# Third token mixer: when its tiles are fetched, which queue issues two of its loads, and which engines copy and scale

## The chip, the cores and the metric

The kernel runs on one core of one Trainium2 chip. The metric is device time in microseconds, the median over runs. The engines that the text names are TensorE (PE), VectorE (DVE), ScalarE (ACT), GpSimd (POOL) and SyncE (SP), which here only issues DMAs. Each engine works through a fixed list of its own instructions in order.

## The reference

Two layers, 512 latent tokens (x) and 256 context tokens (z), width 1024, all in float32. Each layer is a modulated RMSNorm, one wide input projection, three token mixers side by side, gated projections of the three outputs, an output projection and a SwiGLU feed-forward. The change is in the third mixer, a bidirectional recurrence with one 64 x 64 state for each of 8 heads:

```python
def step(S, inp):
    w_t, k_t, v_t, kk_t, a_t = inp[:5]
    sa = jnp.einsum('bhvk,bhk->bhv', S, kk_t)
    S = S * w_t[:, :, None, :] - sa[..., None] * (kk_t * a_t)[:, :, None, :] + v_t[..., None] * k_t[:, :, None, :]
    return S, jnp.einsum('bhvk,bhk->bhv', S, inp[5])
```

It is run over the context first and then over the latent tokens, once forward and once on the reversed sequence; context outputs are needed in the first layer only.

## The kernel before

Matrices stand with features on the partitions. Every float32 product of a large projection is made of three matmuls of a high and a low part (`gemm`); weights come as `raw` tiles from SP, are split into `wh` on ACT and `wl` on DVE (`wunit`), and are used up as "jobs".

The third mixer (`Rwkv.run`) treats the 768 tokens as six stretches of 128 tokens, called halves in the code's words, for each of two directions, `f` and `b`. Two generators ("lanes"), one for a direction, are stepped in turn, and jobs of other work (gates, then the projections of the first two mixers) are put between the steps. For each half and direction there are three stages:

- `prep(d, g)` loads `cp` (log decays), `bk` and `kr` (keys, replacement vectors, receptances) from DRAM over SP, makes cumulative decays (a DVE scan, two ACT exponentials), scales `kr` and `bk` by them (`kr[..., 0:32]` and `bk` on DVE, `kr[..., 32:64]` at L1479 and the final decay `pc` into `bk` at L1498 on POOL), makes score matrices `X` on TensorE, and transposes `bk` into `bkt`.
- `inverse(d, g)` writes parts of `X` to DRAM (`d1`), reads them back as `L`, loads an identity `G`, solves 31 elimination steps of two instructions each (DVE for `f`, POOL for `b`), writes `G` to DRAM (`d2`) and reads it back as `TT`. All these DMAs are SP's.
- `chain(it)` runs four chunks of 32 tokens. For each: `yp` on TensorE from `uv`, `X`, `kr` and the state; `ysb` on ACT; the solve `up` = `TT` times `ysb`; four copies of `up` into `uv`, two on DVE and two on ACT in turn (L1593); `sp` from `uv` and `bkt`; the new state `sblk` on DVE (L1606), for which POOL scaled the old one (`sc`); and, where outputs are needed, `op` and its copy `ys`. The values `uv` come from DRAM over SP, in two loads for each half (L1553).

The first layer runs `prep` and `inverse` one half ahead of the chain, the second two halves ahead (`self.ahead`). The rotating buffers decide when a load may start: `kr` has 6, `cp`, `bk`, `G` and `L` have 2 each for both directions together, `uv` has 2 for each direction. A load into a buffer that is still read waits on its queue, and what stands behind it on that queue waits too.

The code is written in program order, but the order of the instructions on each engine is made by the framework's scheduler at build time, from that order and from its own estimate of times. In the second layer `paced` also ties the jobs' matmuls to the steps of the chain.

Of the kernel before, what the change touches and what calls it, by code (L numbers as in the profile page):

```python
# [20 lines left out]
KD = 8  # L21
# [3 lines left out]
FREE, PER = 150, 3.3  # see paced()  # L25
# [3 lines left out]
class Kern:  # L29
# [18 lines left out]
    # ---------------------------------------------------------------- helpers  # L48
# [35 lines left out]
    def hop(self, i):  # L84
        """a product of a chain that others are paced by"""
        if self.hops is not None:
            self.hops.append(i)

    def paced(self, i, ps):
        """beside a chain: the first FREE products (of 512 columns) as they come, then at most PER more after each one of the chain,  # L90
        so that those of the chain never queue behind many others"""
        if self.hops is not None:
            if self.done >= FREE and self.hops:
                self.after(i, self.hops[min(int((self.done - FREE) / PER), len(self.hops) - 1)])
            self.done += ps.shape[-1] / 512

    def room(self, n):
        """whether n more products fit the pace"""
        return self.done + n <= FREE + PER * len(self.hops)
# [10 lines left out]
    def run_job(self, later=None):  # L110
        """the next queued job; what a job returns is its second half, left to the caller if `later` is a list"""
# [14 lines left out]
    def rsqrt(self, y, s, t):  # L126
        """y = s ** -0.5 (s, y, t: same-shape SBUF tiles)"""
# [7 lines left out]
    def rsqrt_v(self, y, s, t):  # L135
        """y = s ** -0.5 without table functions: a guess from the halved exponent, three Newton steps"""
# [9 lines left out]
    # ---------------------------------------------------------------- consts  # L146
# [32 lines left out]
    # ---------------------------------------------------------------- adaLN  # L179
    def ada(self, l, bank, R, rbufs):  # L180
        """generator: modulation vectors of layer l, one round per 2048 columns; bank(shape, name): a PSUM tile, R: pool of the weights"""
# [36 lines left out]
    # ---------------------------------------------------------------- norm  # L218
    def stats(self, xk, a, b, P, tags, S, y):
        """generator: y <- 1 / rms of the tokens a..b-1 (rows 32 j: j-th quarter); P, tags: PSUM pool and (tag, bufs) of its one-bank tiles;  # L220
        S: pool of temporaries"""
# [18 lines left out]
    def spread(self, y, n, P, tags, S):  # L240
        """the n values of y, over all partitions (PSUM)"""
# [9 lines left out]
    def norm(self, xk, a, b, P, tags, S, apply):  # L251
        """generator: rmsnorm of the tokens a..b-1; apply(k, r): emits what follows for the k-th feature tile, r: 1 / rms over all partitions"""
# [10 lines left out]
    # ---------------------------------------------------------------- mixer input  # L263
    def gemm_x(self, w):
        """one 128-column tile of the input projection of the x tokens, feature-major"""
# [15 lines left out]
    def new_h(self, Z=None):  # L281
        """tiles of the two parts of h; Z: pool of the z tokens, where they lie apart"""
# [3 lines left out]
    def h(self, j, k, a, b):  # L286
        """part j (high, low) of the tokens a..b-1 of h, k-th feature tile"""
        return self.hz[j][k][:, a - NX:b - NX] if self.hz and a >= NX else self.hs[j][k][:, a:b]

    def norm_mod(self, xk, a, b, A, sh, P, tags, S, y=None):  # L290
        """generator: h = rmsnorm(x) * g * (1 + scale) + shift of the tokens a..b-1, split into two float32r parts;
        y: the tokens' 1 / rms, where they are known"""
# [21 lines left out]
    # ---------------------------------------------------------------- layers  # L314
    @contextmanager
    def weights(self, name, bufs, side=None):
        """pool of the weight tiles of the jobs to come; raw ones of their own only at the outermost level"""
# [14 lines left out]
    def fill(self):  # L332
        """one queued job, if any"""
# [6 lines left out]
    def mixed(self, gen, steps, spread):  # L340
        """run the mixer `gen` (about `steps` steps) with the queued jobs spread over it"""
# [9 lines left out]
    def layer(self, l, X, xs):  # L351
# [76 lines left out]
        with self.pool(f"pf{l}", space=PSUM) as pg:  # L428
# [5 lines left out]
            # layer 1: paced by the chain; layer 0, where TensorE is the bound: evenly from the start  # L434
# [30 lines left out]
        # merge, output projection, feed-forward  # L465
# [30 lines left out]
    def branch_jobs(self, l, n):  # L496
        """gated output projections of the first two mixers, summed into accd"""
# [24 lines left out]
    # tokens in two groups: those whose third mixer output comes last (0..127, 384..511) and the others  # L522
# [8 lines left out]
    def branch_operand(self, l, late, raw):  # L531
        """the third mixer's output of one group of tokens, in two parts"""
# [6 lines left out]
    def branch_gemm(self, l, w, m, late, g):  # L539
        """g <- gated product of one group of tokens"""  # L540
# [6 lines left out]
    def last_branch(self, l, n, P):  # L547
        """the third mixer's projection of the first group, added to what accd holds: the first group's operand of the output projection"""
# [18 lines left out]
    def gemm_parts(self, w, nk, rh, rl, parts):  # L567
        """products of the tokens of each part: (PSUM, first token, end)"""
# [51 lines left out]
    def two_parts(self, xs, parts, update, norm, keep=6):  # L620
        """the last KD queued jobs for the first part of the tokens, then for the second, with the first part's norm beside them;
        returns the second part's norm, not yet finished"""
# [25 lines left out]
    def ffn(self, l, n, xs):  # L648
# [3 lines left out]
        with self.ps, self.pool(f"fA{l}") as A:  # L652
# [27 lines left out]
            # the last update in two parts of the tokens, each part's norm as soon as it is there  # L680
# [19 lines left out]
            # the first tiles while the second part's norm is finished  # L700
# [22 lines left out]
    def final(self, xs, a, b, N, S):  # L723
        """generator: the final norm of the tokens a..b-1"""
# [30 lines left out]
# ------------------------------------------------------------------ gated linear attention  # L755
class Gla:
    """one layer's bidirectional gated linear attention; chunks of 128 tokens: x 0..3, z 4..5"""
# [77 lines left out]
    def cum(self, hp):  # L835
        """per-chunk cumulative log gates (times 16) of both directions for head pair hp"""
# [21 lines left out]
    def states(self, hp, B):  # L858
        """scaled queries, and the state before every chunk, of both directions"""
# [164 lines left out]
# ------------------------------------------------------------------ windowed attention  # L1024
class Swa:
    """one layer's grouped-query attention; tile t holds heads t and t + 4, key-value head g the rows 64 g"""

    def __init__(self, K, l, P, ps, yb):
# [13 lines left out]
        # float32r parts: a head's queries as (high; low) in one order of the row halves, keys twice  # L1042
# [5 lines left out]
    def add_jobs(self, P):  # L1048
        """projection jobs; P: pool of what only they need"""
# [46 lines left out]
    def run(self, T):  # L1096
# [4 lines left out]
        # the softmax of one group of heads beside the value products of the group before  # L1101
# [13 lines left out]
    def values(self, T, n, g, keys, r):  # L1115
        """generator: transposes of the weights, value products of one group of heads; its output when both groups are there"""
# [99 lines left out]
# ------------------------------------------------------------------ RWKV-7  # L1216
class Rwkv:
    """one layer's RWKV-7 mixer; tokens: x 0..511, z 512..767; halves of 128 tokens: x 0..3, z 4..5"""
# [9 lines left out]
    def open_f(self):  # L1228
        """what the projection jobs need"""
# [15 lines left out]
        self.hb = P.tile([128, 16], F32, name="hb")  # half of w0 (f p0..3, b p0..3), a0  # L1245
# [43 lines left out]
    # -- evacuation of a projected tile with the centred shift mix  # L1289
# [10 lines left out]
    def add_jobs(self, J, ps, psn):  # L1300
        """projection jobs; J: pool of temporaries, ps/psn: PSUM pool and (tag, bufs) of its one-bank tiles"""
# [14 lines left out]
        def lowrank(half, di, p, t):  # L1316
            """tanh of half the low-rank product plus half the offset"""
# [36 lines left out]
        def keys(p):  # L1354
            """normalised keys, and the two directions' replacement vectors and keys, of head pair p"""
# [67 lines left out]
    def knorm(self, J, bank, big, kt):  # L1423
        """1 / max(|k * k_k|, 1e-12) per head: rows 32 (token block) + head, columns x 0..127, z 128..191"""
# [23 lines left out]
    # -- decays and scores of 128 tokens of one direction  # L1448
    def prep(self, d, g):
        nc, K, T, ps = self.nc, self.K, self.T, self.ps  # L1450
        di = "fb".index(d)
        c4 = slice(4 * g, 4 * g + 4)
        outp = self.need_out(g)
        nI = 64 if outp else 32
# [4 lines left out]
        nc.sync.dma_start(cp.rearrange("q (p c) t -> q p (c t)", c=4), row(self.twd[d]))  # L1459
        nc.sync.dma_start(bk.rearrange("q (p w) c t -> q p (w c t)", w=2), row(self.bkd[d]))  # L1460
        nc.sync.dma_start(kr.rearrange("q (p c) t -> q p (c t)", c=4), row(self.krd))
# [16 lines left out]
        if outp:  # L1478
            nc.gpsimd.tensor_tensor(out=kr[:, :, 32:64], in0=kr[:, :, 32:64], in1=Pi, op=ALU.mult)  # L1479
        yield  # L1480
        # transposed scores, rows (even chunk: B~ j, k~ j; odd chunk: k~ j, B~ j), columns (K~ i, r~ i)
# [14 lines left out]
        v = bk.rearrange("q (p w) (c h) t -> q p (w c) (h t)", w=2, h=2)  # L1496
        for p in range(4):
            nc.gpsimd.tensor_tensor(out=v[:, p], in0=v[:, p], in1=pc[:, p, :].unsqueeze(2).to_broadcast([128, 4, 64]), op=ALU.mult)  # L1498
# [9 lines left out]
    def inverse(self, d, g):  # L1508
# [274 lines left out]
def _layout(x, c, ctx, c_ctx, w_ada, b_ada, g_mix, g_ffn, w_in, w_gk2, b_gk, g_gla, sink, mu_shift, w0, w_w2, a0, w_a2,  # L1783
            w_g2, k_k, k_a, r_k, gn_w, gn_b, w_branch, w_out, w_ffn1, w_ffn3, w_ffn2, g_final):
    f = np.float32
    D = {}
# [74 lines left out]
```

## Time and profile before

| | |
|---|---|
| median of 3 runs | 3359.13 us (3357.03 to 3359.63) |
| profiled execution, first to last instruction | 3361.6 us |
| TensorE busy | 3033.8 us (90%), mean granted clock 0.921 |
| VectorE, ScalarE, GpSimd busy | 1756.6, 1081.2, 990.4 us |
| third mixer, first layer | about 640 to 1165 us of the span |
| third mixer, second layer | about 2436 to 2871 us of the span |

The profiled execution has no time of its own on record other than its span, which stands 2.5 us above the median of the runs. A busy share is a mean over stages; the two stretches of the third mixer have their own.

### The profile page before, as it was taken

Reading aid. Unit: us, or ns where it says so; the run is one execution under the profiler, and the core shown is the slowest. Engines: PE = TensorE matmul, PEld = TensorE weight load, DVE = VectorE, ACT = ScalarE, POOL = GpSimd, SP = SyncE. Lnnn points to the kernel's source line nnn. Section 1 sums busy time; section 2 is a strip of 40 time slices with the busy share of each in tenths; the row PEclk is TensorE's granted clock in tenths of the full one; section 3 lists DMA queues with packets and bytes.
Section 4 is the critical chain, followed back from the end, with each engine's and each line's share of the span. In section 5 each row is a group of like instructions: output and inputs, shape, how many; then the busy total and the mean of one; then the engine's idle time right before and its main releaser. Section 6 shows DMA issues by size and latency. Waiting matters only on the chain. (4 is left out here: it accounts for less than half of the span.)

```text
span 3361.6 us, 62705 instructions
## 1 busy us (share of the span) xinstructions
PE 3033.8 (90%) x25760; PEld 2400.0 (71%) x25760; DVE 1756.6 (52%) x3506; ACT 1081.2 (32%) x2034; POOL 990.4 (29%) x1438
## 2 busy tenths in 40 slices
PE   6999999878889989999999899698857789799998
PEld 3777877666666778888888787576635466788887
DVE  3175557766656755222223454656567566643335
ACT  3255444422222233212122344453322222332223
POOL 2033122344655322101001211312266465221102
PEclk9999999888888999999999899798868679899999
DMA  7421222544345552443212322123633444512223
GB/s 289 153 74 56 96 101 95 174 131 124 99 119 142 168 197 73 153 157 132 63 63 95 96 73 95 58 76 126 205 103 107 112 131 137 187 69 95 96 98 119
DMA packets 269375, 398.33 MB, mean 118 GB/s; under 512 B 94624, under 2 KB 179360, under 8 KB 269088
## 3 DMA queue, kind: packets, MB, share of 16 engines
q1 hardware_dynamic: 249184, 370.20, 34.2%
q10 hardware_dynamic: 19904, 24.12, 2.0%
q8 instruction: 202, 3.31, 0.4%
q14 instruction: 85, 0.70, 0.1%
HBM read 320.33 MB, written 73.92 MB: 117 GB/s over the span
## 5 line engine op out<-in xcount | busy, mean ns | idle before, releaser
L50 PE MATMUL px<-hh,wl 128*128 128x512 f32 x1584 | 646.5, 408 | 31.9 <-DVE wl L72 31.8
L50 PE MATMUL px<-hh,wh 128*128 128x512 f32 x1584 | 651.9, 412 | 14.1 <-ACT wh L71 6.5
L50 PE MATMUL px<-hl,wh 128*128 128x512 f32 x1584 | 643.2, 406 | 11.6 <-POOL hl L302 8.8
L72 DVE TENSOR_TENSOR wl<-raw,wh 128x1024 fp32r<-128x1024 f32 (+1 forms) x314 | 402.3, 1282 | 366.4 <-ACT wh L71 332.1
L71 ACT ACTIVATE wh<-raw 128x1024 fp32r<-128x1024 f32 (+1 forms) x314 | 326.1, 1041 | 778.8 <-PE pz L50 395.2
L50 PEld LDWEIGHTS px<-hh,wl 128*128 128x128 f32 x1584 | 308.2, 195 | 110.0 <-DVE wl L72 38.1
L50 PEld LDWEIGHTS px<-hh,wh 128*128 128x128 f32 x1584 | 309.4, 195 | 106.7 <-issue 24.4
L50 PEld LDWEIGHTS px<-hl,wh 128*128 128x128 f32 x1584 | 308.8, 195 | 82.3 <-POOL hl L302 13.2
L673 POOL TENSOR_TENSOR al<-fs,ah 128x768 fp32r<-128x768 f32 (+1 forms) x44 | 85.0, 1931 | 726.3 <-ACT ah L672 726.3
L50 PE MATMUL pz<-hl,wh 128*128 128x256 f32 x872 | 253.1, 291 | 3.8 <-DVE hl L304 2.0
L50 PE MATMUL pz<-hh,wh 128*128 128x256 f32 x872 | 253.5, 292 | 1.5 <-DVE fs L663 1.4
L50 PE MATMUL pz<-hh,wl 128*128 128x256 f32 x872 | 252.0, 289 | 1.3 <-DVE wl L72 0.8
L50 PEld LDWEIGHTS pz<-hl,wh 128*128 128x128 f32 x872 | 171.2, 196 | 10.4 <-POOL hl L302 2.6
L50 PEld LDWEIGHTS pz<-hh,wh 128*128 128x128 f32 x872 | 170.3, 196 | 11.2 <-issue 3.2
L50 PE MATMUL px<-y,wh 128*128 128x512 f32 (+1 forms) x512 | 155.8, 391 | 24.8 <-ACT y L123 10.0
L50 PEld LDWEIGHTS pz<-hh,wl 128*128 128x128 f32 x872 | 170.4, 195 | 7.0 <-issue 5.2
L1532 POOL TENSOR_TENSOR ftmp<-G,L 128x60 f32<-128x60 f32 (+24 forms) x372 | 125.9, 338 | 146.9 <-DMA G<-gid 55.8
L1532 DVE TENSOR_TENSOR ftmp<-G,L 128x60 f32<-128x60 f32 (+24 forms) x372 | 107.4, 289 | 103.8 <-DMA G<-gid 55.6
L1533 POOL TENSOR_TENSOR G<-G,ftmp 128x60 f32<-128x60 f32 (+24 forms) x372 | 131.4, 353 | 25.2
L50 PE MATMUL sp<-uv,bkt 64*64 64x64 f32 x1536 | 99.8, 249 | 36.9 <-DVE uv L1593 36.5
L50 PEld LDWEIGHTS px<-y,wh 128*128 128x128 f32 x512 | 96.1, 209 | 44.2 <-ACT y L123 12.5
L50 PEld LDWEIGHTS sp<-uv,bkt 64*64 64x64 f32 x1536 | 69.3, 147 | 75.4 <-DVE uv L1593 41.1
(443 smaller groups left out, 6090.9 us busy)
## 6 DMA issues: line engine op xcount, KB each, us to landing
raw<-win SPq DMA_DIRECT2D x114, 512.0 KB
raw<-w SPq DMA_DIRECT2D x104, 512.0 KB
araw<-wada SPq DMA_DIRECT2D x96, 512.0 KB
raw<-w SPq DMA_DIRECT2D x48, 448.0 KB
kr<-krd SPq DMA_DIRECT2D x24, 512.0 KB
L<-d SPq DMA_DIRECT2D x24, 512.0 KB
gs<-gat ACTq DMA_DIRECT2D x24, 384.0 KB
raw<-wab SPq DMA_DIRECT2D x16, 512.0 KB
```

What stands on the lines that cost most here:

```text
L50: return self.nc.tensor.matmul(out, lhsT=lhsT, rhs=rhs, start=start, stop=stop)
L71: nc.scalar.activation(h[:, :n], raw[:, :n], AF.Copy)
L72: nc.vector.tensor_tensor(out=lo[:, :n], in0=raw[:, :n], in1=h[:, :n].bitcast(F32), op=ALU.subtract)
L673: nc.gpsimd.tensor_tensor(out=al, in0=s, in1=ah.bitcast(F32), op=ALU.subtract)
L1532: eng.tensor_tensor(out=t, in0=G[:, rows, j:j + 1].to_broadcast([128, a, m]), in1=L[:, j:j + 1, cols].to_broadcast([128, a, m]), op=ALU.mult)
L1533: eng.tensor_tensor(out=G[:, rows, cols], in0=G[:, rows, cols], in1=t, op=ALU.subtract)
```

## The change

`load` takes the three loads out of `prep`. The first half's loads stand at the start of `run`, the later ones in `inverse` of the half before, behind its `L`; `kr` now goes ahead of `bk`. `load_v` takes the `uv` loads out of `chain`, one window of 64 tokens at a time, after the first and the third chunk of each half, and issues them from ACT's queue. `G` is loaded from ACT's queue too. All four copies of `up` are ACT's. The two scalings that were POOL's for both directions are DVE's for `f` and POOL's for `b`, and the scaling by `pc` is one instruction where it was four. The diff also drops comments and docstrings.

```diff
+    def load(self, d, g):
+        nc, T = self.nc, self.T
         c4 = slice(4 * g, 4 * g + 4)
         cp = T.tile([128, 16, 34], F32, name="cp", tag="cp", bufs=2)
         kr = T.tile([128, 16, 64], F32, name="kr", tag="kr", bufs=6)
         bk = T.tile([128, 8, 4, 32], F32, name="bk", tag="bk", bufs=2)
         row = lambda a: a[:, :, c4, :].rearrange("q p c t -> q p (c t)")
         nc.sync.dma_start(cp.rearrange("q (p c) t -> q p (c t)", c=4), row(self.twd[d]))
+        nc.sync.dma_start(kr.rearrange("q (p c) t -> q p (c t)", c=4), row(self.krd))
         nc.sync.dma_start(bk.rearrange("q (p w) c t -> q p (w c t)", w=2), row(self.bkd[d]))
-        nc.sync.dma_start(kr.rearrange("q (p c) t -> q p (c t)", c=4), row(self.krd))
+        self.loaded[d, g] = cp, kr, bk
+    def load_v(self, d):
+        if self.windows[d]:
+            g, w = self.windows[d].popleft()
+            uv = self.uvs[d, g, w] = self.T.tile([128, 4, 2, 64], F32, name="uv", tag="uv" + d, bufs=2)
+            v0 = 128 * g + 64 * w
+            self.nc.scalar.dma_start(uv[32:96].rearrange("q p e v -> q (p e v)"), self.vtok[v0:v0 + 64, :])
     def prep(self, d, g):
+        eng = nc.vector if d == "f" else nc.gpsimd
+        cp, kr, bk = self.loaded.pop((d, g))
...
         if outp:
-            nc.gpsimd.tensor_tensor(out=kr[:, :, 32:64], in0=kr[:, :, 32:64], in1=Pi, op=ALU.mult)
+            eng.tensor_tensor(out=kr[:, :, 32:64], in0=kr[:, :, 32:64], in1=Pi, op=ALU.mult)
...
-        v = bk.rearrange("q (p w) (c h) t -> q p (w c) (h t)", w=2, h=2)
-        for p in range(4):
-            nc.gpsimd.tensor_tensor(out=v[:, p], in0=v[:, p], in1=pc[:, p, :].unsqueeze(2).to_broadcast([128, 4, 64]), op=ALU.mult)
+        v = bk.rearrange("q a (c h) t -> q (a c) (h t)", h=2)
+        eng.tensor_tensor(out=v, in0=v, in1=pc.rearrange("q p c -> q (p c)").unsqueeze(2).to_broadcast([128, 16, 64]), op=ALU.mult)
...
-    def inverse(self, d, g):
+    def inverse(self, d, g, later):
...
+        if later is not None:
+            self.load(d, later)
         G = T.tile([128, 8, 32], F32, name="G", tag="G", bufs=2)
-        nc.sync.dma_start(G, self.I["gid"])
+        nc.scalar.dma_start(G, self.I["gid"])
...
     def chain(self, it):
-        uvs = {}
-        for w in ((0, 1) if d == "f" else (1, 0)):
-            uv = uvs[w] = T.tile([128, 4, 2, 64], F32, name="uv", tag="uv" + d, bufs=2)
-            v0 = 128 * g + 64 * w
-            nc.sync.dma_start(uv[32:96].rearrange("q p e v -> q (p e v)"), self.vtok[v0:v0 + 64, :])
...
             for p in range(4):
-                o, i_ = uv[ru, p].rearrange("q e v -> q (e v)"), up[32 * p:32 * p + 32, :]
-                (nc.scalar.copy if p % 2 else nc.vector.tensor_copy)(o, i_)
+                nc.scalar.copy(uv[ru, p].rearrange("q e v -> q (e v)"), up[32 * p:32 * p + 32, :])
...
+            if n % 2 == 0:
+                self.load_v(d)
...
     def run(self):
+        for d in "fb":
+            self.load(d, seqs[d][0])
+            self.windows[d] = deque((g, w) for g in seqs[d] for w in ((0, 1) if d == "f" else (1, 0)))
+        for d in "fb":
+            self.load_v(d)
```

Two places show how the scheduler's order moves. The first is SP's list in the second layer, around the end of the chain's first half. The `kr` rows here load the fourth half of each direction and wait until the chain has left the first half; `d2` and `TT` are the way of the second half's solves, forward first (in the rows of before `TT_23584` and `TT_23601`). Before:

```order
L1461 DMA kr_24337<-krd1_20782 128x4x256
L1518 DMA L_23828<-d1_23824 128x1x1024
L1461 DMA kr_24373<-krd1_20782 128x4x256
L1536 DMA d2_23456<-G_23467 4x256x32
L1459 DMA cp_25061<-twdf1_20783 128x4x136
L1518 DMA L_23863<-d1_23859 128x1x1024
L1536 DMA d2_23462<-G_23486 4x256x32
L1553 DMA uv_24317<-vtok1_20789 64x512
L1538 DMA TT_23584<-d2_23456 128x8x32
L1521 DMA G_23923<-gid 128x256
```

Now, from the corresponding stretch of the changed kernel, where `TT_23552` and `TT_23569` are the second half's:

```order
L1532 DMA L_23774<-d1_23770 128x1x1024
L1552 DMA d2_23412<-G_23429 4x256x32
L1554 DMA TT_23552<-d2_23412 128x8x32
L1532 DMA L_23809<-d1_23805 128x1x1024
L1552 DMA d2_23418<-G_23454 4x256x32
L1554 DMA TT_23569<-d2_23418 128x8x32
L1457 DMA kr_23870<-krd1_20746 128x4x256
L66 DMA raw_24459<-win 128x1024
L1457 DMA kr_23935<-krd1_20746 128x4x256
```

Both `TT` loads now stand directly behind their `d2` writes (one `L` between the two pairs), with no `uv`, `cp` or `G` between them; the two waiting `kr` loads moved behind them.

The second place is ACT's list in the second layer at the chain's first chunk, where the first copies of `up` stand. Before:

```order
L1505 COPY bkt_23728<-tp_23818 128x512
L1505 COPY bkt_23794<-tp_23847 128x512
L1593 COPY uv_23603<-up_23663 32x128 x2
L1505 COPY bkt_23794<-tp_23853 128x512
L1593 COPY uv_23633<-up_23729 32x128
L1467 ACTIVATE cp_24372<-cs_24378 128x544
L1593 COPY uv_23633<-up_23729 32x128
L1574 ACTIVATE ysb_23808<-yp_23795 128x128
```

Now, with the `G` loads of the second half's solves ahead of the copies:

```order
L1537 DMA G_23429<-gid 128x256
L1482 ACTIVATE cp_23869<-cs_24294 128x544
L1537 DMA G_23454<-gid 128x256
L1483 ACTIVATE cs_24294<-cs_24294,lnh_65 128x544
L1603 COPY uv_22801<-up_23611 32x128 x4
L1603 COPY uv_22803<-up_23676 32x128 x4
L1585 ACTIVATE ysb_23754<-yp_23741 128x128
```

All eight copies of a chunk pair are ACT's now, and DMA issues that may wait for a buffer (`G_23429` and `G_23454` take the buffers of the first half's `G`, once `d2` has been written from them) stand in the same list.

## Rows read from the trace of the kernel before

**Rows 1.** The page's first line.

```profile
span 3361.6 us, 62705 instructions
```

**Rows 2.** Windows: stretch, length, busy PE, PEld, DVE, ACT, POOL, PE clock, DMA.

```profile
640.00:1165.00 525.00, 458.54 (x5954) 342.68 (x5951) 327.10 (x807) 138.14 (x330) 262.07 (x541) 0.88 0.46 134
2436.00:2871.00 435.00, 343.45 (x4621) 231.82 (x4619) 270.99 (x703) 104.67 (x259) 244.32 (x524) 0.76 0.41 116
2774.00:2845.00 71.00, 70.96 (x1080) 46.48 (x1082) 42.11 (x101) 19.50 (x56) 34.03 (x59) 0.93 0.42 135
```

**Rows 3.** Waits of PE, 640 to 1165: us in total, times, longest.

```profile
PE sp L50 <- DVE uv L1593: 31.6, 7, 8.7
PE px L50 <- DVE wl L72: 11.6, 9, 6.7
PE xp L50 <- DVE bk L1477: 10.0, 2, 5.6
...
PE up L1584 <- DMA TT<-d: 3.7, 2, 2.1
```

**Rows 4.** Waits of PE, 2436 to 2871.

```profile
PE up L1584 <- DMA TT<-d: 27.4, 4, 16.2
PE px L50 <- DVE wl L72: 17.7, 4, 10.8
PE xp L50 <- POOL kr L1479: 11.9, 2, 7.3
...
PE up L1584 <- ACT ysb L1574: 5.0, 2, 4.8
```

**Rows 5.** Timeline of SP's queue, second layer: start, us until issued, instruction.

```profile
2541.50 0.58 SPq L1536 DMA_DIRECT2D d<-G  x1
...
2553.30 8.73 SPq L1553 DMA_DIRECT2D uv<-vtok  x1
2562.12 0.53 SPq L1538 DMA_DIRECT2D TT<-d  x1
```

**Rows 6.** Timeline of SP's queue, a hundred us later.

```profile
2661.76 0.54 SPq L1536 DMA_DIRECT2D d<-G  x1
2673.60 0.39 SPq L1538 DMA_DIRECT2D TT<-d  x1
```

**Rows 7.** Waits on SP's queue, 640 to 1165.

```profile
SPq L1553 <- PE op L1611: 50.2, 15, 12.8
SPq L1538 <- DMA d<-G: 40.7, 11, 11.5
```

**Rows 8.** Waits on SP's queue, 2436 to 2871.

```profile
SPq L1538 <- DMA d<-G: 35.1, 9, 11.2
...
SPq L1553 <- PE op L1611: 22.7, 6, 10.1
```

**Rows 9.** Waits of DVE, 2436 to 2871.

```profile
DVE ftmp L1532 <- DMA G<-gid: 42.9, 4, 21.0
```

**Rows 10.** Tile uv: its copies and loads, ns min/median/max.

```profile
L1593 DVE COPY uv<-up x192: 268/284/292, 738.5 to 2864.0; 32x128 f32<-32x128 f32 x192
L1593 ACT COPY uv<-up x192: 254/257/262, 738.8 to 2864.3; 32x128 f32<-32x128 f32 x192
L1553 SPq DMA_DIRECT2D uv<-vtok x48: 494/554/8792, 656.6 to 2823.2; - x48
```

**Rows 11.** Tile kr: its two scalings, ns min/median/max.

```profile
L1475 DVE TENSOR_TENSOR kr<-kr,cp x24: 674/686/2140, 655.2 to 2710.4; 128x512 f32<-128x512 f32 x24
L1479 POOL TENSOR_TENSOR kr<-kr,cp x20: 1176/1218/2158, 653.0 to 2711.2; 128x512 f32<-128x512 f32 x20
```

**Rows 12.** Tile bk: its two scalings.

```profile
L1498 POOL TENSOR_TENSOR bk<-bk,pc x96: 607/612/1678, 661.0 to 2730.1; 128x256 f32<-128x256 f32 x96
L1477 DVE TENSOR_TENSOR bk<-bk,cs x24: 1206/1228/2221, 653.7 to 2658.2; 128x1024 f32<-128x1024 f32 x24
```

**Rows 13.** Waits of POOL, 640 to 1165.

```profile
POOL kr L1479 <- ACT cp L1467: 27.4, 4, 10.7
```

More of the change, by code (lines that the diff above doesn't have):

```diff
@@ L1446, in need_out @@
         return g < 4 or self.zout
-    def prep(self, d, g):
-        nc, K, T, ps = self.nc, self.K, self.T, self.ps
-        di = "fb".index(d)
+    def load(self, d, g):
+        nc, T = self.nc, self.T
         c4 = slice(4 * g, 4 * g + 4)
-        outp = self.need_out(g)
-        nI = 64 if outp else 32
         cp = T.tile([128, 16, 34], F32, name="cp", tag="cp", bufs=2)
@@ L1459, in prep @@
         nc.sync.dma_start(cp.rearrange("q (p c) t -> q p (c t)", c=4), row(self.twd[d]))
+        nc.sync.dma_start(kr.rearrange("q (p c) t -> q p (c t)", c=4), row(self.krd))
         nc.sync.dma_start(bk.rearrange("q (p w) c t -> q p (w c t)", w=2), row(self.bkd[d]))
-        nc.sync.dma_start(kr.rearrange("q (p c) t -> q p (c t)", c=4), row(self.krd))
+        self.loaded[d, g] = cp, kr, bk
[5 more added lines that the diff above has]
+            self.nc.scalar.dma_start(uv[32:96].rearrange("q p e v -> q (p e v)"), self.vtok[v0:v0 + 64, :])
+    def prep(self, d, g):
+        nc, K, T, ps = self.nc, self.K, self.T, self.ps
+        di = "fb".index(d)
+        eng = nc.vector if d == "f" else nc.gpsimd
+        outp = self.need_out(g)
+        nI = 64 if outp else 32
+        cp, kr, bk = self.loaded.pop((d, g))
         flat = lambda a: a.rearrange("q a b -> q (a b)")
@@ L1556, in chain @@
             w, q = cl // 2, cl % 2
-            S, uv = self.st[d], uvs[w]
+            S, uv = self.st[d], self.uvs[d, g, w]
             rv = slice(32, 64) if q == 0 else slice(64, 96)
@@ L1667, in run, with front @@
         done, tails = set(), []
-        def front(d, g):
-            yield from self.prep(d, g)
-            yield from self.inverse(d, g)
+        self.loaded, self.windows, self.uvs = {}, {}, {}
+        def front(d, i):
+            yield from self.prep(d, seqs[d][i])
+            yield from self.inverse(d, seqs[d][i], seqs[d][i + 1] if i < 5 else None)
+        seqs = {d: [g for x, g in self.ORDER if x == d] for d in "fb"}
+        for d in "fb":
[3 more added lines that the diff above has]
+            self.load_v(d)
         def lane(d):
-            seq = [g for x, g in self.ORDER if x == d]
+            seq = seqs[d]
             for i in range(self.ahead):
-                for _ in front(d, seq[i]):
+                for _ in front(d, i):
                     yield
             for i, g in enumerate(seq):
-                nxt = front(d, seq[i + self.ahead]) if i + self.ahead < 6 else iter(())
+                nxt = front(d, i + self.ahead) if i + self.ahead < 6 else iter(())
                 it = dict(d=d, g=g, ys=None)
```

## Prediction

> **What bounds the kernel now.** I read the windows over the two stretches of the third mixer first, then who TensorE waits for in each, then the SP queue, since SP is what the change touches most. In the first layer the mixer takes 525 us, of which TensorE is idle 525.0 - 458.5 = 66.5, at a mean granted clock of 0.88; in the second it takes 435 us, idle 91.5, clock 0.76 [rows 2]. The reader is to see that both stretches have TensorE as the engine that does most, and that in neither is it full: 158 us of idle time in all. A third row says where the floor is: from 2774 to 2845, when no half border and no front of a later half is in the way, TensorE is busy 70.96 of 71 us. There a faster chain would buy nothing. So the change can win only what waits cost elsewhere, and the slower clock that comes with them.
>
> The waits of TensorE have different ends. In the first layer the largest is `sp` behind the DVE copies of `up`, 31.6 us in 7 places [rows 3]: the copy itself is 0.28 us [rows 10], so DVE was held by something else in its list. In the second layer it is `up` behind the landing of `TT`, 27.4 us in 4 places, the longest 16.2, which is the start of the chain [rows 4]. Behind `TT` stands SP. At one border of halves `d2` was issued at 2541.5 and `TT` at 2562.1 [rows 5]; at another place, with nothing between them, the same pair is 11.84 us apart, and that is what the write to DRAM takes until it is seen [rows 6]. So at the first place `TT` could have gone at 2541.5 + 11.84 = 2553.3, and it went 8.8 us later; the row between them is a `uv` load that sat 8.73 us on SP for its buffer.
>
> **What the change removes.** The `uv` loads leave SP. Their waits there for `op` are 50.2 us in 15 places in the first layer and 22.7 in 6 in the second [rows 7, 8]; most are hidden, because what stands behind them is not due. By rows 4 I count what is not: of the 27.4 us of `TT` the 16.2 stay (the first half's solve has no chain before it to hide in), the other 11.2 go, since `TT` now stands directly behind `d2`. In the first layer, of 3.7, I take 2.
>
> *DMA: Bandwidth & Descriptors* of the Trainium skill, section "Issuing engines are not separate DMA queues", says that starting DMAs from several engines saves only the sequencer's time to initiate them, usually small beside the DMA. The trace shows something else on this queue, the wait in rows 5, which is 16 times the median issue of 0.554 us in rows 10. By the page the move is worth nothing on the path and its place in the sum would be 0 where I have 13.2.
>
> The copies leave DVE. With four in turn on two engines they cost 2 x 0.284 + 2 x 0.257 = 1.08 us a chunk, on ACT alone 4 x 0.257 = 1.03 [rows 10]: nothing by themselves. What goes is the wait on a held DVE. But the state update that follows is DVE's too, so it is still late; only the copy and `sp` come out from under it. I take half of the 31.6 us of the first layer, 16; all of it would be the upper bound, 0 the lower. In the second layer, 5 for `ysb` and the like [rows 4].
>
> The scalings move. For `f`, 12 halves lose 4 x 0.612 = 2.45 us each on POOL and 10 lose 1.218, in all 41.6 us; DVE gets 12 x 1.228 + 10 x 0.686 = 21.6 us (priced by its own scalings of the same shapes) and loses 192 x 0.284 = 54.5 [rows 10 to 12]. ACT gets 192 x 0.257 = 49.3 us and 72 DMA issues, at SP's 0.554 us 40 at most. DVE has 525 - 327 and 435 - 271 us of room, ACT more [rows 2], so the moved work is hidden. What counts is that POOL, in order, stood at `f`'s work: `kr` there waited 27.4 us for ACT's exponentials [rows 13] with `b`'s solve behind it. In the second layer TensorE waits 11.9 us for that same POOL instruction [rows 4]; the load under it still waits for a buffer, so I take half, 6.
>
> *SBUF — State Buffer* of the Trainium skill, section "Who interferes with whom", says that a DVE instruction with two SBUF inputs and a GpSimd instruction that reads SBUF contend, one blocking until the other ends. That speaks against giving `f`'s products to DVE while POOL solves `b`. The trace agrees that such pairs stretch: 1.228 us becomes 2.221 at worst, 0.612 becomes 1.678 [rows 12]. By the page the 22 new DVE instructions could cost up to 22 x (1.678 - 0.612) = 24 us, an estimate, and the sum would be 42 instead of 66.
>
> In the sum I take 0 for this stretching: 22 instructions come on DVE and 12 x 4 + 10 = 58 go on POOL. Its bounds are 0 and 24.
>
> The loads a half ahead: the rows of order show that the scheduler had already put `kr`, `cp` and `bk` as early as their buffers allowed, and the buffers are as many as before. I take 0 for `xp` behind `bk` (10.0, [rows 3]), between 0 and 10. For `px` behind `wl` (11.6 and 17.7, [rows 3, 4]), weights on a held SP or DVE, 3 in each layer; the one wait of 10.8 I put down to `G`, and it stays.
>
> **What stays, and what is late next.** `G` needs the buffer that `d2` is written from, wherever it is issued, so DVE's 42.9 us of waits for it [rows 9] stay. After the `uv` waits the next in line is that write: 75.8 us in 20 places on SP [rows 7, 8].
>
> **The sum.** First layer: 2 + 16 + 3 = 21. Second: 11.2 + 5 + 6 + 3 = 25. Together 46 us of 158 idle. The clock: 0.12 x 458.5 + 0.24 x 343.5 = 137 us are lost to the lower of its two levels, 1.2 instead of 2.4 GHz, of which 0.88 and 0.76 are means [rows 2]. In rows 2 the clock is lower where more is idle; with 46 of 158, 29%, of the idle gone I expect 40 back at most, and take half, 20, as the chain, not TensorE, is last in part of that time. Sum 66. The rows are of an execution with a span of 3361.6 [rows 1], 2.5 above the median of 3359.1; against the median that is 3293.
>
> **Rivals.** (1) *Only issue time is saved.* What is late is the round trip through DRAM, 11.84 us from `d2` to `TT` [rows 6], and every wait that I remove uncovers it. For it: 9 of the second layer's SP waits are that landing, and 35.1 us against 22.7 for `uv` [rows 8]. Against it: rows 5, where 8.8 us come on top. Then the time is unchanged, 3352 to 3366. This is what the page on DMA of the Trainium skill, cited above, would have.
>
> (2) *Half of it.* The held DVE delays the state update as it delayed the copy, so the 16 go to 0, and the clock does not come back: 66 - 16 - 20 = 30, so 3329 (3319 to 3349).
>
> (3) *Much more.* All `sp` waits go (16 more), the 10 for `bk`, the rest of `kr` and `wl` (6 and 14, less the 10.8 of `G`, so 9), and the clock comes back in full with 87 of 158, 75 us: 46 + 41 + 75 = 162 at the extreme, 3197; more likely around 3240.
>
> (4) *Slower: ACT becomes the queue that is held.* `G` now stands on ACT ahead of copies and `ysb`, and waits for the `d2` write. 24 such waits (6 halves, 2 directions, 2 layers) at the mean of 75.8 / 20 = 3.8 us [rows 7, 8] are 91 us, at the full 11.84 us 284. It decides against the change once more than the 66 us are lost on the path: 17 of 24 at the mean, 6 of 24 at the full wait. For it: the order puts both `G` of the next half ahead of the first copies. Against it: `up` ahead of those copies needs `TT`, which waits for the same write and then has its own load to do. With 9 full waits: 107 - 66 = 41 slower, 3400.
>
> **Chances.** My forecast (35 to 110 us faster) 0.47; much more 0.13; half 0.18; unchanged 0.08; slower 0.14. Predicted is the first, 3293. A range of 3215 to 3358 leaves out most of the slower case, part of the unchanged one and the far end of the third, some 0.2. Within 0.2%, 6.7 us, a measurement of this kernel can't tell a difference; faster 0.78, same 0.08, slower 0.14. The forecast's own range is 3249 to 3324.
>
> **What would show it.** Right: `TT` some 12 us behind `d2` at every border; TensorE's `sp` waits in the first layer at about 16 us, `up` waits in the second at about 16; both stretches shorter by 25 to 40 us, with clocks of 0.9 and above 0.8; POOL some 40 us less busy. Wrong: DMA issues on ACT that last microseconds with `ysb` or copies behind them (rival 4); idle time of TensorE that only changes its name to `sblk`, `L` or `G` (rivals 1, 2). What I can least see is how the scheduler's new order, made of its own times, meets the real ones: in the second layer a solve's end and the next one's start stand close together, and each such pair costs DVE the full round trip.

## The result and the profile after

The changed kernel takes 3393.23 us (median of 4 runs, 3384.44 to 3404.08), the kernel before 3359.38 beside it: a ratio of 1.0098, with a 95% interval of 1.0072 to 1.0123. That is 34 us slower, where the prediction was 66 faster; its range ended at 3358.

The page of the changed kernel begins with the span and the busy time of each engine; the span was 3361.6 [rows 1].

```profile
span 3394.7 us, 62575 instructions
...
PE 3014.1 (89%) x25760; PEld 2403.8 (71%) x25760; DVE 1725.6 (51%) x3336; ACT 1126.2 (33%) x2226; POOL 942.1 (28%) x1344
```

The windows of the same two stretches (columns as in rows 2):

```profile
640.00:1176.00 536.00, 446.73 (x5914) 341.63 (x5910) 310.58 (x724) 157.32 (x423) 237.22 (x493) 0.82 0.45 128
2456.00:2900.00 444.00, 331.43 (x4682) 230.75 (x4680) 256.23 (x623) 131.11 (x360) 228.06 (x485) 0.77 0.42 118
```

TensorE is idle for 89 us in the first stretch and 113 in the second, where it was 66.5 and 91.5 [rows 2], and the clock of the first fell from 0.88 to 0.82. The work did move as meant: DVE and POOL are less busy, ACT more. So the loss is waiting. Who TensorE waits for, first layer (total, times, longest):

```profile
PE up L1595 <- DMA TT<-d: 17.2, 1, 17.2
PE up L1595 <- ACT ysb L1585: 9.4, 3, 6.0
PE yp L1580 <- DVE sblkb L1616: 9.0, 4, 6.2
...
PE op L1601 <- ACT ys L1623: 8.8, 3, 6.0
PE ty L1669 <- ACT bkt L1519: 5.5, 1, 5.5
```

and second layer:

```profile
PE px L50 <- DVE wl L72: 23.9, 11, 7.6
PE up L1595 <- DMA TT<-d: 22.6, 1, 22.6
PE up L1595 <- ACT ysb L1585: 16.3, 4, 6.0
PE yp L1580 <- DVE sblkb L1616: 11.2, 4, 4.8
...
PE tp L1518 <- POOL bk L1512: 9.4, 1, 9.4
```

The 31.6 us of `sp` behind DVE's copies [rows 3] are gone. In their place stand ACT's `ysb`, `ys` and `bkt`, DVE's `sblk`, and one wait of 17.2 us for `TT` that was 2.1 at its longest. That one is the start of the chain. SP's queue there, in the kernel before (start, us until issued):

```profile
715.92 0.56 SPq L1536 DMA_DIRECT2D d<-G  x1
716.52 8.79 SPq L1460 DMA_DIRECT2D bk<-bkdf  x1
...
727.26 0.39 SPq L1538 DMA_DIRECT2D TT<-d  x1
```

and in the changed kernel:

```profile
725.78 0.55 SPq L1552 DMA_DIRECT2D d<-G  x1
729.10 7.57 SPq L1532 DMA_DIRECT2D L<-d  x1
736.72 0.52 SPq L1552 DMA_DIRECT2D d<-G  x1
737.34 10.11 SPq L1458 DMA_DIRECT2D bk<-bkdf  x1
747.49 0.61 SPq L1554 DMA_DIRECT2D TT<-d  x1
```

In both, what stands directly behind a `d2` write takes 7 to 10 us to be issued. Before, `TT` stood behind one such issue, 11.3 us behind its `d2`; now the second direction's `d2` comes first, there are two, and `TT` is 21.7 us late. Over the whole kernel 9 issues on SP last over 5 us before (78.7 us in all) and 9 after (73.6): all behind a `d2` write but one, behind a `TT` load. Whichever transfer stood there paid, among them `bk`, `cp`, `kr`, `L`, `raw`, `TT`, and `uv` in rows 5.

At the place of rows 5 the changed kernel does what the prediction wanted, with `TT` next behind `d2` and 12.7 us after it, where it was 20.6:

```profile
2557.74 0.55 SPq L1552 DMA_DIRECT2D d<-G  x1
2570.45 0.38 SPq L1554 DMA_DIRECT2D TT<-d  x1
```

ACT at the start of the first layer's chain (in brackets the idle time before an instruction and what ended it):

```profile
726.15 0.60 ACT L1519 COPY bkt<-tp 128x512 f32<-128x512 f32 x1
738.63 0.34 ACTq L1537 DMA_DIRECT2D G<-gid  x1
739.01 1.07 ACT L1519 COPY bkt<-tp 128x512 f32<-128x512 f32 x2 [12.26 <-DMA d<-G]
749.46 0.35 ACTq L1537 DMA_DIRECT2D G<-gid  x1
```

The first `G` waits until `d2` has landed, with two copies of `bkt` behind it, and the second does it again. For each of the 24 `G` loads I took the time from the end of ACT's instruction before it to its issue: 20 stand over half a microsecond, 133.6 us in all. The groups that touch `G` list who waited for that; of ACT (us, times):

```profile
  ACT cp L1482: 20.1, 4
  ACT cs L1483: 17.2, 2
  ACT bkt L1519: 12.3, 1
  ACT ys L1623: 11.6, 2
  ACT uv L1603: 9.4, 1
...
  ACT ysb L1585: 6.7, 1
```

Milestones say where the 33.1 us of the span came in (us from the span's start, `TT` at the end of its first issue, chain end at the last state update; the runs e1 to c1 are told in the next section):

| | cp, layer 1 | first d2 | first TT | chain end | cp, layer 2 | first d2 | first TT | chain end | span |
|---|---|---|---|---|---|---|---|---|---|
| before | 638.1 | 715.9 | 727.7 | 1160.4 | 2392.7 | 2479.3 | 2499.6 | 2870.4 | 3361.6 |
| changed | 639.0 | 725.8 | 748.1 | 1171.7 | 2413.0 | 2504.5 | 2525.2 | 2899.1 | 3394.7 |
| e1, G on SP | 641.1 | 724.8 | 739.7 | 1174.2 | 2413.9 | 2507.2 | 2520.2 | 2902.7 | 3397.3 |
| e6, d2 in rows | 640.6 | 727.0 | 737.2 | 1159.6 | 2400.8 | 2493.7 | 2503.3 | 2884.8 | 3381.8 |
| c2, both | 641.7 | 728.3 | 739.8 | 1154.7 | 2392.9 | 2487.4 | 2497.0 | 2860.3 | 3353.9 |
| c1, on before | 636.5 | 712.7 | 726.0 | 1126.6 | 2370.0 | 2458.5 | 2468.1 | 2838.9 | 3335.1 |

In the first layer the start loses 20 us and the chain wins 9 back (432.7 to 423.6 from `TT` to its end). Another 9 come between the mixers, 5 at the second layer's start, 3 in its chain, 4 behind it. These are single executions; n1, whose order is that of before, differs from it by up to 2.5 us in such a length.

SP's holds are only half of the first start's 20 us. From `cp` to the first `d2` it takes 86.8 us where it took 77.8, since the first solve of `f` on DVE lasts 37.6 us and not 28.6, with more of DVE's other work inside it. The split of the scalings isn't needed for that: in s1, which moves none, the solve lasts 38.1. The second layer's 5 us, too, stand wholly ahead of its first `d2` (91.5 us against 86.6).

### The profile page after: what moved, and what is told of

The parts are those of the page before. It is cut to its first block, busy times and chain, and to the rows that moved or that the text cites. A ratio compares the mean times of both kernels' runs of the same rounds, so it can differ in the third digit from the quotient of the medians.

```text
span 3394.7 us, 62575 instructions
## 1 busy us (share of the span) xinstructions
PE 3014.1 (89%) x25760; PEld 2403.8 (71%) x25760; DVE 1725.6 (51%) x3336; ACT 1126.2 (33%) x2226; POOL 942.1 (28%) x1344
## 5 line engine op out<-in xcount | busy, mean ns | idle before, releaser
L50 PE MATMUL px<-y,wh 128*128 128x512 f32 (+1 forms) x512 | 152.6, 386 | 31.6 <-ACT y L123 14.1
L1548 POOL TENSOR_TENSOR ftmp<-G,L 128x60 f32<-128x60 f32 (+24 forms) x372 | 133.2, 358 | 165.8 <-DMA L<-d 78.7
L1603 ACT COPY uv<-up 32x128 f32<-32x128 f32 x384 | 98.2, 256 | 68.0 <-PE up L1595 50.7
L50 PE MATMUL px<-ah,wh 128*128 128x512 f32 x296 | 116.1, 393 | 0.0
```

The lines of the kernel that those rows point to most:

```text
L50: return self.nc.tensor.matmul(out, lhsT=lhsT, rhs=rhs, start=start, stop=stop)
L1548: eng.tensor_tensor(out=t, in0=G[:, rows, j:j + 1].to_broadcast([128, a, m]), in1=L[:, j:j + 1, cols].to_broadcast([128, a, m]), op=ALU.mult)
L1603: nc.scalar.copy(uv[ru, p].rearrange("q e v -> q (e v)"), up[32 * p:32 * p + 32, :])
```

## The experiments

Each ran beside the kernel before on the same chip; differences are of those medians. The first four take one part of the change back.

**e1: G on SP again.**

```diff
-        nc.scalar.dma_start(G, self.I["gid"])
+        nc.sync.dma_start(G, self.I["gid"])
```

> The changed kernel with one edit: G is loaded from SP's queue again. Theory A (ACT is the held queue): in the changed kernel ACT stands 134 us in 20 places at G's load, until the write of d2 has landed, with bkt copies, ysb and copies of up behind it; with G on SP these holds go, and most of the 34 us that were lost come back: 3360 to 3370 us, ACT's ysb and uv waits of TensorE (9.4 and 16.3 us for ysb) gone. Theory B (SP is held behind every d2 write for 8 to 10 us, and what counts is what the new order puts there): the time stays at 3385 to 3400, since TT f still stands behind d2 b and bk at the chain's start. If both hold, in between: the later start (18 us in layer 1) stays and the waits for ysb go, 3372 to 3380.

3399.16 us against 3365.95, ratio 1.0091 (1.0073 to 1.0109): nothing comes back. By the milestones `TT` comes 10 and 6 us sooner after `cp`, and the two chains take 11 and 9 longer. Theory A alone falls.

**e2: the copies on two engines again** (`nc.scalar.copy` in turn with `nc.vector.tensor_copy`).

> The changed kernel with one edit: the copies of up alternate between DVE and ACT again. Theory A (ACT held by G): two of the four copies of each chunk leave the held queue but the other two stay, so nearly nothing comes back, 3385 to 3395; TensorE's sp waits for DVE's uv (31.6 us in layer 1 before) return in part and may cost 10 more, 3395 to 3405. If instead ACT's own load (copies 1.08 us a chunk) were the cost, 5 to 15 us come back: 3378 to 3388.

3420.28, 1.0156 (1.0136 to 1.0176): 21 us worse than with the copies on ACT. That is beyond all three ranges. The copies are worth having there.

**e3: both scalings on POOL again**, `pc` in four instructions.

> The changed kernel with one edit: the two scalings are POOL's for both directions again, the one by pc in four instructions. If the split by direction costs (DVE's f solve takes 37.3 us instead of 28.3 in the first half of layer 1, with bk, kr and X inside, and one POOL instruction of 1.9 us delays tp by 9.4 us in layer 2), 10 to 15 us come back: 3378 to 3385. Theory A or B: it changes nothing beyond the scheduler's own shifts, 3388 to 3400.

3406.24, 1.0115 (1.0097 to 1.0132), above both ranges: taking the split back returned nothing.

**e4: the loads in `prep` again.**

> The changed kernel with one edit: cp, bk and kr are loaded in prep, in the old order, and not one half ahead. If the loads ahead are what put bk between d2 and TT at the chain's start (theory B, in which TT f is 21.7 us behind its d2 instead of 11.3), 10 to 18 us come back: 3375 to 3383. Theory A (G on ACT): unchanged, 3388 to 3400, since the start's 12 us of ACT behind G stay.

3410.79, 1.0129 (1.011 to 1.0147), above both ranges: nothing comes back here either.

The next four are the last part taken back, and single edits to the kernel before.

**e5: uv as it was.** The two `load_v` calls at the start of `chain`, on SP. Theory C is that the moved `uv` loads cost the 34 us; theory D, that no part costs by itself, but any edit gives another order than that of before.

> The changed kernel with the uv loads as they were: both windows at the start of a chain's half, from SP's queue. Theory C: the 34 us come back, 3355 to 3372. Theory D: it stays slower than before by 20 to 50 us, 3385 to 3415, as the four other parts did when they were taken back alone.

3388.58 against 3365.06, 1.0076 (1.0053 to 1.01): 10 us of the 34 at most, so theory C falls.

**s1: only the uv loads, early and from ACT**, on the kernel before.

> The kernel before with one part of the change: the uv loads, one window at a time behind the first and third chunk, from ACT's queue. Theory C (this part is what costs the change its 34 us, since none of the other four, taken back alone, returned them): 3385 to 3400. Theory D (no part costs by itself: the scheduler makes another order on every engine with any edit, and the order of before happens to meet the real times well): also slower, 3375 to 3400, but so are the other single parts of this call. The prediction's own step (uv leaves SP, TT stands directly behind d2): 3340 to 3355.

3394.37, 1.009 (1.0069 to 1.0111): 29 us slower, where the prediction counted this as the gain for `TT`. It leaves theory D possible.

**s2: only the copies on ACT.**

```diff
-                (nc.scalar.copy if p % 2 else nc.vector.tensor_copy)(o, i_)
+                nc.scalar.copy(o, i_)
```

> The kernel before with one part of the change: all four copies of up on ACT. The prediction's step (the 31.6 us of sp behind DVE's uv go, half of them are won): 3340 to 3352. Theory C: no loss from this part, 3340 to 3366. Theory D: 3375 to 3400, as with any other edit.

3357.77, 0.9975 (0.9961 to 0.9989), 7 us faster, short of the prediction's step. With it falls theory D as it was put: not every edit slows the kernel. The waits of TensorE in the first layer show why not more:

```profile
PE sp L50 <- DVE sblkf L1606: 27.2, 4, 11.9
PE tp L1504 <- DVE G L1533: 13.2, 1, 13.2
PE yp L1569 <- DVE sblkb L1606: 12.0, 6, 7.6
```

DVE is as late as it was; TensorE now waits for its state update where it waited for its copy.

**s4: kr loaded ahead of bk.** Two lines swapped, no work changed.

> The kernel before with the two loads kr and bk swapped in the code, nothing else: no engine gets more or less work, and both are waited for by the same stage. Theory D (the order made at build time is what decides): the lists of all engines change, and the time with them, 3375 to 3400. Theory C, and any theory in which a part costs by its work or its waits: 3360 to 3372, no change.

3379.59, 1.0058 (1.0036 to 1.0079): 14.5 us slower.

**s5: only the split scalings, and s6: only the loads one half ahead**, on the kernel before.

> The kernel before with one part of the change: the scalings of kr and bk on DVE for f and on POOL for b, the one by pc in one instruction. The prediction's step (6 us of kr off POOL in the second layer): 3352 to 3362. Theory E (any edit moves the order, as the swap of kr and bk did with +14.5 us, and this counts for more than the work moved): 3370 to 3395.

> The kernel before with one part of the change: cp, bk and kr (in the old order) issued one half ahead, from inverse. The prediction's step (0, since the buffers are as many): 3360 to 3368. Theory E: 3370 to 3395, with as many bytes and as many instructions on each engine.

s5: 3428.98 against 3368.44, 1.0192 (1.0164 to 1.022), 61 us slower, the dearest edit of all and beyond theory E's range. The new instructions themselves cost what was counted: DVE's scaling by `pc` has a median of 1.212 us here and a longest of 1.301. What grew is the time in which DVE stands, over the first layer:

```profile
DVE ftmp L1532 <- DMA L<-d: 46.2, 4, 16.2
DVE bk L1477 <- DMA bk<-bkdf: 44.2, 4, 25.0
```

23.0 and 31.7 (longest 12.2) they were in the kernel before over the same length. s6: 3388.32, 1.006 (1.004 to 1.008), 20 us slower with the same loads and the same instructions.

**f6 and e6: d2 in rows**, in the kernel before and in the changed one. The write was in pieces of 32 floats; now each partition's 256 floats go in one piece, and the load of `TT` does the gathering it did already.

```diff
-        d2 = self.D.tile([8, 4, 32, 32], F32, name="d2", tag="d2", bufs=3)
+        d2 = self.D.tile([4, 8, 4, 8, 32], F32, name="d2", tag="d2", bufs=3)
-        nc.sync.dma_start(d2.rearrange("m p (a s) i -> s (m p) a i", s=4), G)
+        nc.sync.dma_start(d2.rearrange("s m p a i -> (s m p) a i"), G)
-        nc.sync.dma_start(TT, d2.rearrange("m p r i -> (p r) m i"))
+        nc.sync.dma_start(TT, d2.rearrange("s m p a i -> (p a) s m i"))
```

> The kernel before with d2 laid out in DRAM as G lies on the partitions, so that the write has one piece of 1 KB for each partition where it had eight of 128 bytes; the load of TT still gathers 128 bytes at a time. The result is the same. Theory B (SP is held for 4 to 10 us by what comes behind a d2 write, because of that write): the holds of 7 to 10 us behind d2 vanish, TT comes less than 8 us behind d2 where it was 11.8, and the time falls by 10 to 40 us, 3325 to 3355, unless the order made at build time takes it back. If the hold is not the write's but a buffer's, as the prediction had it: the holds stay, 3355 to 3370.

> The changed kernel with the same other layout of d2. Theory B: the holds go, and with them ACT's 134 us behind G shrink by a third or more; the time falls by 15 to 45 us from 3393 to 3399, so 3350 to 3380. If ACT and SP were held by something else: unchanged, 3385 to 3400.

f6: 3356.74 against 3368.44, 0.9967 (0.9951 to 0.9983), 12 us faster. e6: 3377.37, 1.0031 (1.0015 to 1.0048), where the changed kernel had 1.0098. SP's queue in f6, at the place shown above:

```profile
718.53 0.48 SPq L1536 DMA_DIRECT2D d<-G  x1
719.05 0.55 SPq L1460 DMA_DIRECT2D bk<-bkdf  x1
...
729.95 0.61 SPq L1538 DMA_DIRECT2D TT<-d  x1
```

`bk` is issued in 0.55 us where it took 8.79. Of the 9 long issues one is left in f6 (6.8 us, behind a `TT` load) and none in e6. No `uv` load takes over 1.70 us in f6, where three took 8.4 to 8.8. So the write in small pieces held the queue, as theory B had it, and no buffer did. The rest of theory B came out only in part. f6's time lies just outside its 3325 to 3355 and inside the range of the other reading, so it is the queue's rows that decide. `TT` at the place shown is 11.4 us behind its `d2`, as before: there the hold of `bk` was hidden behind the landing of the write. At the place of rows 5 it is 10.2 us behind, where it was 20.6. ACT's standing at `G` fell by a quarter in e6, from 133.6 to 101.8 us.

**c0: split and copies together**, on the kernel before.

> The kernel before with two parts of the change: the scalings split by direction, and all copies on ACT. Alone they gave about +61 and -7 us. Theory F (the split is dear because DVE then has f's scalings, f's solve and half the copies in one list, and the copies' move is what makes room): the pair comes to 0 to +25, 3365 to 3390. If the parts add up: +54, 3415 to 3425.

3390.57 against 3363.65, 1.0081 (1.0055 to 1.0107): 27 slower, a little beyond what theory F gave and half of what the parts would add up to. Beside the copies on ACT the split still costs 34.

**c1: copies on ACT and d2 in rows**, on the kernel before.

> The kernel before with all copies on ACT and d2 in rows. Alone they gave -7 and -12 us. If the two causes (DVE held at the copies, SP held behind d2) are each won, about -19: 3340 to 3352. Theory E (the order made at build time moves the time by some 15 us at any edit): anywhere from 3340 to 3375.

3343.7, 0.9934 (0.9911 to 0.9958): 20 us faster than before, as the two gains add up. Its windows of the two stretches:

```profile
640.00:1130.00 490.00, 431.09 (x5890) 328.07 (x5888) 296.24 (x709) 156.93 (x419) 257.73 (x539) 0.87 0.48 139
2414.00:2840.00 426.00, 317.98 (x4616) 219.89 (x4616) 244.71 (x610) 127.81 (x355) 243.74 (x524) 0.78 0.43 118
```

The first stretch is 35 us shorter than in rows 2, the second 9. Not all of that is won, since TensorE is busy for 27 and 25 us less in them: between the mixers 11 us are added, and behind the second 5.

**n1: the two writes of d1 the other way round, and s3: only G on ACT.**

> The kernel before with the two writes of d1 in the other order, which changes no engine's work and no wait that the code asks for. Theory E: the lists of all engines come out otherwise, and the time lies 5 to 25 us from the kernel before, on either side. If an order of its own has no price and the +14.5 us of the swap of kr and bk were those loads' own: 3362 to 3370, no change.

> The kernel before with one part of the change: G loaded from ACT's queue. Rival 4 of the prediction (ACT is held by G until d2 has landed): 3385 to 3410, and ACT stands over 100 us at G. If such holds are hidden, as the changed kernel with G back on SP says (3399 against 3393): 3360 to 3372.

n1: 3365.84, 1.0009 (0.999 to 1.0027), no change. Its lists came out row for row as before, against what was expected, so it tells only that the same order gives the same time. s3: 3395.73, 1.0098 (1.0062 to 1.0134), 32 us slower. ACT stands 134.3 us at `G` in 20 places, here with `ysb` behind it:

```profile
2636.13 0.37 ACTq L1521 DMA_DIRECT2D G<-gid  x1
2636.60 0.28 ACT L1574 ACTIVATE ysb<-yp 128x128 f32<-128x128 f32 x1 [11.96 <-DMA d<-G]
...
2655.47 0.38 ACTq L1521 DMA_DIRECT2D G<-gid  x1
2655.89 0.28 ACT L1574 ACTIVATE ysb<-yp 128x128 f32<-128x128 f32 x1 [9.07 <-DMA d<-G]
```

**n3: the copy of pc two instructions later, and c2: the changed kernel with G on SP and d2 in rows.**

> The kernel before with DVE's copy of pc (0.17 us, 24 of them) written two instructions further down in prep. No engine's work changes. Unlike the swap of d1's writes, which left every engine's list as it was (and the time, +2 us), this edit moves 456 of DVE's 3510 rows and 2165 of TensorE's 19282. Theory E (the order made at build time has a price of its own, of 10 to 30 us): at least 7 us from the kernel before, on either side. If order alone has no such price and only the parts' waits count: 3358 to 3370.

> The changed kernel with G back on SP and d2 in rows, which takes both holds away that were found: ACT's behind G and SP's behind d2. With d2 in rows alone it took 3377 (0.3% above before). If G on ACT costs in the changed kernel what it costs alone (+33), and e1 hid this behind SP's holds: 3345 to 3360, faster than before. If the price of G on ACT is that of another order: 3370 to 3390.

n3: 3387.33 against 3366.48, 1.0056 (1.0037 to 1.0076), 21 us slower without a change of work. So another order made at build time has a price, and of the two such edits that I tried, s4 and n3, both were dearer than the order of the kernel before. c2: 3353.11, 0.996 (0.9944 to 0.9976): 13 us faster than before. Its windows:

```profile
640.00:1160.00 520.00, 445.28 (x5930) 341.25 (x5928) 312.01 (x730) 160.62 (x426) 238.63 (x495) 0.84 0.46 133
2436.00:2862.00 426.00, 319.44 (x4623) 221.55 (x4623) 259.99 (x627) 129.69 (x357) 225.70 (x485) 0.78 0.43 120
```

Against e6 the two starts are 1.5 us longer each and the chains 7.5 and 18 shorter. I put that down to `G` on ACT, which held copies and `ysb` in the chain, but the order changed with the edit too.

## Why the prediction was wrong

**The cause.** In ratios to the kernel before, the changed kernel goes from 1.0098 to 1.0031 with `d2` in rows and to 0.996 with `G` on SP as well: 0.67% and 0.71%, 23 and 24 us, together more than the 34 lost. Here both holds had to go: with `G` alone back (e1) SP is still held behind `d2`, and what the starts win the chains lose again. The traces show both holds, and that each goes with its edit. How much of the 34 us each of them cost is less sure, as every edit but n1 also changed the order, and order alone was worth up to 21 us. And `d2` in rows wins 12 us in the kernel before as well (f6, 0.9967): beside it, what is left of the change in c2 (0.996) wins nothing that can be told.

**TT behind uv on SP (2 + 11.2).** This step failed at its reading of rows 5, "a `uv` load that sat 8.73 us on SP for its buffer". It sat there because the second direction's `d2` write had gone 0.7 us before it (at 2552.6), a row that the order ahead of the prediction shows and rows 5 leave out. In f6, with fewer pieces in that write, no `uv` issue takes over 1.70 us. The Trainium skill's page *Perfetto Trace Analysis*, section "DMA Instruction — HWDGE (DVE, Sync)", says that the profiled time of an issue begins when its semaphores are satisfied and covers the making of the descriptors. By that an issue of 8.73 us is no wait for a buffer, and f6 agrees. The waits for buffers are those of rows 7 and 8, which stand in rows of their own.

The forecast 11.2 us did go: in the second layer TensorE waits for `TT` once, at the start, where it waited four times. But in the new order two held issues stand ahead of the first layer's first `TT`, and the waits at the two starts grew, from 2.1 to 17.2 us and from 16.2 to 22.6. All waits for `TT` together went from 31.1 to 39.8 us. The second start's growth isn't SP's: from `d2` to `TT` it takes 20.7 us there and took 20.3.

**The 11.84 us of rows 6** are one case and no fixed price. In the kernel before 8 pairs of `d2` and `TT` have nothing between them on SP, and they lie between 4.7 and 13.8 us. All 24 pairs, taken in order, lie between 4.7 and 20.6 (230.2 in all), and in f6 between 1.7 and 12.7 (157.6).

**Copies (16).** The mechanism was right, the size wasn't: s2 measured 7 for the whole edit, between my 16 and rival 2's 0, since DVE's state update is late where its copy was.

**ysb, kr and wl (5 + 6 + 3 + 3).** `kr` on POOL is gone from the waits, and one `tp` behind POOL's `bk` of 9.4 us stands there now. `wl` grew from 17.7 to 23.9 in the second layer, and `ysb` from 5.0 [rows 4] to 16.3. All four of these waits are for a `ysb` that stands behind a `G` in ACT's list, as here:

```profile
2570.45 0.40 ACTq L1537 DMA_DIRECT2D G<-gid  x1
2570.89 0.28 ACT L1585 ACTIVATE ysb<-yp 128x128 f32<-128x128 f32 x1 [6.75 <-DMA d<-G]
```

**G stays (0).** It did, but its wait moved onto the queue that has `ysb` and all copies. Rival 4 named this and its place, with 91 us of standing at the mean and 3400 for the time; it was 133.6 us, and 3393. Alone (s3) it cost 32. I gave it 0.14 because `up` "waits for the same write and then has its own load to do". That holds for the half whose `d2` it is; in the chain the copies and `ysb` that stood behind `G` were another half's or the other direction's.

**Scalings (0).** Alone 61, beside the copies 34. The stretching that I took at nothing is there, on the other engine. In the changed kernel DVE's twelve by `pc` keep their length, 1.208 to 1.274 us, but beside 7 of them a step of POOL's solve takes 1.10 to 1.40 us, where the shortest of its shape takes 0.22 to 0.33:

```profile
706.50 1.36 POOL L1548 TENSOR_TENSOR ftmp<-G,L 128x50 f32<-128x50 f32 x1
706.52 1.21 DVE L1512 TENSOR_TENSOR bk<-bk,pc 128x1024 f32<-128x1024 f32 x1
```

POOL's solves together grew from 257.3 to 270.2 us, inside the bounds of 0 and 24 and too little for 61 or 34. What stands out beside it is that f's instructions wait in DVE's list for loads, with f's solve behind them; how much of the cost that is and how much is order, I can't tell.

**Loads ahead (0).** 20 alone, about what the two edits that change no work cost, 14.5 and 21. With these sizes the single parts can't be told from the order that came with them, and they don't add up: +29, -7, +61, +20 and +32 alone make 135, and the change has 34.

**The clock (20).** I tied it to the idle time. That grew in both stretches, and the clock fell in the first layer, 0.88 to 0.82, but not in the second, 0.76 to 0.77. So nothing came of this term, and the tie itself isn't shown.

**A sum.** In rival 3 the 14 for the rest of `wl` leaves out the first layer's 8.6, so its extreme should be some 9 us further off.

**What stays open.** Why taking back a single part never returned more than 10 us; why the first `d2` still comes 9 and 8 us later after `cp` than before when both holds are gone (c2); and which rows of an order carry its price. `G` with four buffers, which might take its wait away wherever it is issued, wasn't tried.

## What to carry to other kernels

A load that takes long to be issued may be paying for the transfer in front of it: look at that one's pieces before moving the load, since here whatever came next paid. A wait that is moved to another queue still costs what stands behind it there, so choose the queue by that and not by how idle its engine is. And where a scheduler makes the order, measure two or three edits that change no work: here such an edit was worth up to 21 us, and a gain estimated below that can't be forecast from waits alone.

## What the runs showed of the hardware

A DRAM write of 1024 pieces of 128 bytes held its queue. In the kernel before 15 of the 24 such writes had another issue on SP within 3.5 us: 9 of these took 7 to 10 us and 6 took 1.3 to 3.8. In f6, where the same bytes go in 128 pieces, none of the 24 next issues took over 0.78. While SP was held so in the changed kernel (737.34 to 747.45), ACT issued `G` at 738.63 in 0.34 us, so the hold is the queue's.

Twelve DVE products of two SBUF operands kept their length, beside POOL's solve too, but the step of POOL beside one of them didn't: 1.36 us at 706.50, where the next step, of the same shape, took 0.28. In the kernel before others of DVE's were the ones to stretch, to 2.140 and 2.221 us [rows 11, 12].
